# The second feed-forward product as 2x2x2 blocks with seven products

## The chip, the cores and the metric

The kernel runs on one core of one Trainium2 chip. The metric is device time in microseconds (us) of one execution, the median of several. Engine names are those of the profile: PE (matrix products), PEld (its weight loads), DVE (VectorE), ACT (ScalarE), POOL (GpSimd), SP (the engine that issues the DMAs).

## The reference

The reference computes one step of a two-layer streaming model on 1024 prompt tokens and 64 sample tokens, which the kernel puts side by side as T = 1088 columns. Layer 0 has a state-space mixer, layer 1 a banded attention that also makes shared keys and values. Behind each mixer stands the same gated feed-forward network, and the change lies in its second product, `... @ w_out`:

```python
def swiglu(u, w_in, w_out):
    g, up = jnp.split(u @ w_in, 2, axis=-1)
    return (jax.nn.silu(g) * up) @ w_out
...
        xp = xp + rmsnorm(swiglu(rmsnorm(xp, nw[2]), ffn_w_in[layer], ffn_w_out[layer]), nw[3])
```

The width of the model is 1024 (8 tiles of 128), the hidden width 2816 (FT = 22 tiles of 128).

## The kernel before

Activations lie with features on the 128 partitions and tokens in the columns. A float32 operand is split into a high part, rounded to the matrix engine's float32r format, and the low rest; a product is three matmuls (high by high, high by low, low by high). Tokens are cut in two ways: three slices SL of 384, 384 and 320 columns, and four quarters QS of 256, 256, 288 and 288. Two quarters make a half: b = 0 with 512 columns, b = 1 with 576.

`back` is everything behind a mixer's output, once per layer. Its first product (`plain_pairs`, `run_pair`) is already computed by blocks: for a pair of weight tiles (gate and up) and a half b, `run_pair` makes seven products P1 to P7 on operands of one quarter's width (256 columns for b = 0, 288 for b = 1). VectorE adds the results up from PSUM (L1328 to L1345), ScalarE takes the SiLU, GpSimd multiplies (L1342, L1346), and the hidden tile is written to the DRAM tensor `hd` (hscr in the rows). First come 6 pairs of half 0 without blocks, then 16 pairs with both halves, then 6 pairs with half 1 alone.

The second product is plain. For each slice s and each of 8 output tiles m it adds up 22 hidden tiles k, with three matmuls each (L1514 to L1516), in one PSUM tile. `loader` reads each hidden tile back from `hd` into a staging tile `sg` and splits it (ScalarE copies the high part, L1376; VectorE subtracts, L1377) into cells of the rings RX and R. The weights come through `Weights`: a DMA into one of two `raw` tiles or one tile lent from RX (L252), a ScalarE copy (L342), a VectorE subtraction (L343) into one of three `hl` tiles, which the matmuls read. An item of this plan is 8, 8 or 6 tiles of 128 columns. A `raw` tile can be loaded again when its item is split, and an `hl` tile is free again when its item's matmuls are done, so that the three `raw` and the three `hl` tiles form a ring.

At the end of a slice `end` scales (L1430), adds the residual from DRAM (x1d or x3d, L1386; L1431) and writes out. In layer 0 it then splits the result into the operands u of the next stage (L1447, L1448), sums squares (L1453 to L1455) and makes the slice's normalising row `rba`. The keys, queries and values of layer 1 (projections through `unit`, L467 to L469, two PSUM tiles `mm`) come next, slice by slice: V, K and Q of slices 0 and 1, K of a second head pair on both, and then slice 2. Their results leave PSUM through VectorE (L1679 vt, L1626 kf, L1652 qf).

PE's order is that of the program text, in which small generator tasks (`st.spawn`) are placed at estimated times. On the other engines and on SP a list scheduler fixes one static order, from priorities (`tc.high_priority`) and its own estimates; each engine then takes its instructions in that order.

## Time and profile before

| what | value |
|---|---|
| runs | 2938.93, 2940.55 and 2941.53 us (median 2940.55) |
| span of the profiled execution | 2929.9 us |
| outside the span, median less span | 10.65 us |
| first product, layer 0 and layer 1 | 912.7 to 1315.4 and 2250.1 to 2653.6 us |
| second product, layer 0 and layer 1 | 1315.4 to 1580.3 and 2653.6 to 2916.4 us |

The page gives no time of its own for the profiled execution besides the span, from the first instruction to the last; it is taken to have the same 10.65 us around it as the median run. A row of the view of stretches ("windows") has the stretch, its length, and for each engine the busy time and in brackets the number of instructions, then the granted clock of PE, the share of time in which the DMA engines were busy, and GB/s. A row of a view of groups has line, engine, operation, out<-in, shape and count, then busy time in us and mean ns of one, then idle time before them and what ended it. A row of DMA issues ends with KB each and the median us from issue to landing.

### The profile page before, as it was taken

What the parts mean: (1) busy time and instruction counts of PE and PEld (TensorE: products, weight loads), DVE (VectorE), ACT (ScalarE), POOL (GpSimd) and SP (SyncE); (2) the same over time, 40 slices, a digit from 0 to 9 for tenths busy, and PEclk for the clock granted to TensorE, in tenths of its full rate; (3) what the DMA queues carried; (4) which work ended last, traced back from release to release, by engine and by line L of the source; (5) the groups of instructions that cost most, each with busy time, mean ns of one, the idle gap of its engine ahead of it and who ended that gap; (6) DMA issues with size and microseconds to landing.
All of it is one profiled execution on the core that took longest, in us unless ns stands there. A gap on an engine that the chain in (4) does not pass through costs nothing.

```text
span 2929.9 us, 56271 instructions
## 1 busy us (share of the span) xinstructions
PE 2897.3 (99%) x21562; PEld 2858.7 (98%) x21562; DVE 2027.6 (69%) x4452; ACT 1403.6 (48%) x2535; POOL 718.9 (25%) x884
## 2 busy tenths in 40 slices
PE   8999999999999999999999999999999999999999
PEld 8999999999999999999999899999999999999998
DVE  7988878885867555583567887778688554575544
ACT  6655546454544222353445665556664222244443
POOL 1333333331022434350111000000131434351111
PEclk9999999999999999999999999999999999999999
DMA  4423333335564222345664322223476222245654
GB/s 138 133 92 106 104 98 109 100 117 165 165 187 137 76 81 77 108 151 163 207 192 154 98 74 72 65 69 108 132 204 179 83 77 81 75 154 178 225 171 135
DMA packets 203422, 369.12 MB, mean 126 GB/s; under 512 B 20752, under 2 KB 149488, under 8 KB 203152
## 3 DMA queue, kind: packets, MB, share of 16 engines
q1 hardware_dynamic: 199920, 354.97, 38.3%
q0 software_dynamic: 3232, 10.56, 2.0%
q8 instruction: 169, 2.77, 0.4%
q14 instruction: 101, 0.83, 0.1%
HBM read 298.24 MB, written 62.74 MB: 123 GB/s over the span
## 4 chain that ended last, share of the span: by engine, by line
PE 88%; DVE 6%; DMA 2%; ACT 2%; issue 1%; SPq 0%; POOL 0%; DVEq 0%; ACTq 0%; POOLq 0%
PE px L1314 9%; PE px L1315 9%; PE px L1313 9%; PE mm L467 8%; PE mm L469 8%; PE mm L468 8%; PE po L1515 6%; PE po L1516 6%; PE po L1514 6%; PE mmx L468 3%; PE mmx L469 3%; PE mmx L467 3%; PE ptp L1747 2%; PE po L1782 2%; PE S L1716 1%
## 5 line engine op out<-in xcount | busy, mean ns | idle before, releaser
L467 PE MATMUL mm<-r,hl 128*128 128x384 f32 (+2 forms) x1704 | 566.6, 333 | 2.6 <-DVE vt L1679 1.0
L469 PE MATMUL mm<-r,hl 128*128 128x384 f32 (+2 forms) x1704 | 549.6, 323 | 1.0 <-DVE hl L343 0.7
L468 PE MATMUL mm<-r,hl 128*128 128x384 f32 (+2 forms) x1704 | 549.3, 322 | 0.0
L343 DVE TENSOR_TENSOR hl<-raw,hl 128x1024 fp32r<-128x1024 f32 x216 | 256.3, 1187 | 216.6 <-ACT hl L342 208.9
L1314 PE MATMUL px<-r,hl 128*128 128x288 f32 (+1 forms) x1184 | 347.6, 294 | 0.0
L467 PEld LDWEIGHTS mm<-r,hl 128*128 128x128 f32 x1704 | 321.9, 189 | 4.9 <-DVE vt L1679 1.3
L469 PEld LDWEIGHTS mm<-r,hl 128*128 128x128 f32 x1704 | 321.1, 188 | 1.9 <-DVE hl L343 1.0
L468 PEld LDWEIGHTS mm<-r,hl 128*128 128x128 f32 x1704 | 322.2, 189 | 0.3
L1315 PE MATMUL px<-r,hl 128*128 128x288 f32 x1056 | 311.5, 295 | 0.0
L1313 PE MATMUL px<-r,hl 128*128 128x288 f32 x1056 | 310.4, 294 | 0.0
L342 ACT CAST hl<-raw 128x1024 fp32r<-128x1024 f32 x216 | 216.8, 1004 | 162.5 <-PE po L1516 101.6
L493 POOL TENSOR_TENSOR ssum<-ssum,sq 128x256 f32<-128x256 f32 (+3 forms) x97 | 125.5, 1295 | 616.9 <-ACT sq L492 601.3
L1314 PEld LDWEIGHTS px<-r,hl 128*128 128x128 f32 x1184 | 222.4, 188 | 0.0
L1315 PE MATMUL px<-rx,hl 128*128 128x256 f32 x768 | 214.2, 279 | 3.6 <-DVE hl L343 3.5
L1313 PE MATMUL px<-rx,hl 128*128 128x256 f32 x768 | 213.9, 278 | 0.4 <-DVE x L1290 0.4
L1515 PE MATMUL po<-rx,hl 128*128 128x384 f32 (+1 forms) x624 | 202.0, 324 | 0.2
L1313 PEld LDWEIGHTS px<-r,hl 128*128 128x128 f32 x1056 | 198.9, 188 | 0.1
L1315 PEld LDWEIGHTS px<-r,hl 128*128 128x128 f32 x1056 | 198.9, 188 | 0.0
L1514 PE MATMUL po<-rx,hl 128*128 128x384 f32 (+1 forms) x608 | 197.7, 325 | 0.0
L1516 PE MATMUL po<-rx,hl 128*128 128x384 f32 (+1 forms) x608 | 196.7, 324 | 0.0
L1314 PE MATMUL px<-rx,hl 128*128 128x256 f32 x640 | 178.4, 279 | 0.0
L1514 PE MATMUL po<-r,hl 128*128 128x384 f32 (+1 forms) x448 | 148.4, 331 | 0.0
(367 smaller groups left out, 7890.1 us busy)
## 6 DMA issues: line engine op xcount, KB each, us to landing
raw<-in_w_f_dram SPq DMA_DIRECT2D x154, 512.0 KB, 3.7
rx<-in_w_f_dram SPq DMA_DIRECT2D x54, 512.0 KB, 3.7
raw<-in_w_in_dram SPq DMA_DIRECT2D x40, 512.0 KB, 3.7
MT<-ascr SPq DMA_DIRECT2D x48, 384.0 KB, 4.3
sg<-hscr SPq DMA_DIRECT2D x88, 192.0 KB, 3.4
raw<-in_w_f_dram SPq DMA_DIRECT2D x44, 384.0 KB, 3.2
raw<-in_w_so_dram SPq DMA_DIRECT2D x32, 512.0 KB, 3.7
raw<-in_w_o_dram SPq DMA_DIRECT2D x19, 512.0 KB, 3.6
```

What stands on the lines that cost most here:

```text
L342: self.nc.scalar.copy(h, v)
L343: (eng or self.eng or self.nc.vector).tensor_tensor(lo, v, h, op=ALU.subtract)
L467: PE.matmul(ps[:, :n], h_, xh, start=(first and i == 0), stop=False)
L468: PE.matmul(ps[:, :n], h_, xl, start=False, stop=False)
L469: PE.matmul(ps[:, :n], l_, xh, start=False, stop=(last and i == nk - 1))
L493: (eng or G).tensor_tensor(ssum[:, :n], ssum[:, :n], q[:, :n], op=ALU.add)
L1313: PE.matmul(ps, wh, ah[:, k, :], start=(k == 0), stop=False)
L1314: PE.matmul(ps, wh, al[:, k, :], start=False, stop=False)
L1315: PE.matmul(ps, wl, ah[:, k, :], start=False, stop=(k == 3))
L1514: PE.matmul(ps[:, :n], wh, xh, start=(k == 0), stop=False)
L1515: PE.matmul(ps[:, :n], wh, xl, start=False, stop=False)
L1516: PE.matmul(ps[:, :n], wl, xh, start=False, stop=(k == FT - 1))
```

## The change

The second product is made by blocks too. The hidden tiles are paired: i and i + 11 (HF = 11) are the two halves of the inner dimension, even and odd output tiles the two halves of the output, and the two quarters of a half b those of the columns. Seven products (PROD2) with 11 inner tiles each and 4 output pairs g replace eight; P1, P6, P2 and P7 run on both halves with one load of the weights, P5, P4 and P3 on half 0 and then, with the weights loaded again, on half 1. `gate2` adds the PSUM results up in four SBUF tiles yq that hold the whole output.

The sums of hidden blocks are made in the first product, while the tiles are still in SBUF (`sum_one`, `sum_two`: four VectorE operations for each pair of tiles and half), and written to a new DRAM tensor hsm (hsum). The sums of weight blocks are made there too (`load_sums`, `sum_weights`: 24 jobs of four VectorE operations on 256 or 128 columns, two jobs at a time, loaded into z or an R tile and written to wsm, wsum). An order edge puts these sums behind a PSUM addition on VectorE and the weight loads behind the sums' DMAs on SP. In the second product the hidden tiles are loaded into their cells without a staging tile. A weight item is now 5 or 6 tiles; the low part of the item with 5 is made on GpSimd, the other on VectorE. The end works by quarters (`end`), and `end_slice` makes the operands of the next stage from two quarters.

```diff
+HF = FT // 2
+ORD = [i + HF * e for i in range(HF) for e in range(2)]
...
+WCH = ((6, 5), (0, 6))
...
-        for s in range(NSL):
-            for m in range(KD):
-                for k0, nk in KCH:
-                    W.plan(dict(src=[w2[m][:, k0 * P:(k0 + nk) * P]], n=nk * P))
-
-    KCH = ((0, 8), (8, 8), (16, 6))
...
+        for p_, x, y, _ in PROD2:
+            for g in range(4):
+                for k0, nk in WCH:
...
+                    W.plan(dict(src=[src], n=nk * P, eng=k0 > 0 and nc.gpsimd))
...
+    PROD2 = [
+        (P1, (0, 0), None, (0, 1)), (P6, None, 0, (0, 1)), (P2, (1, 0), None, (0, 1)), (P7, None, 3, (0, 1)),
+        *[(p_, x, y, (b,)) for b in range(2) for p_, x, y in ((P5, None, 2), (P4, None, 1), (P3, (1, 1), None))],
+    ]
...
+            def sum_weights(w, last):
...
+                for to, x, y, op in ((b22, b22, b12, SUB), (b12, b12, b11, SUB), (b11, b22, b11, ADD), (b21, b21, b11, SUB)):
+                    behind(V.tensor_tensor(to, x, y, op=op), last)
+                nc.sync.dma_start(wsm[:, :, g, c:c + n], z)
...
+            def sum_one(b, i, got, last=None):
...
+                behind(V.tensor_tensor(y0, got[0, 0], got[0, 1], op=SUB), last)
+                W.behind = nc.sync.dma_start(hsm[:, 0, i, BO[b] // 2:BO[b] // 2 + n], y0)
...
+                for j, to, x, y, op in ((2, y0, a22, y0, SUB), (1, y1, a21, a22, ADD), (3, y3, a12, y0, SUB)):
+                    behind(V.tensor_tensor(to, x, y, op=op), last)
+                    W.behind = nc.sync.dma_start(hsm[:, j, i, BO[b] // 2:BO[b] // 2 + ops[b].n], to)
...
+            for p_, _, _, bs in PROD2:
+                for g in range(4):
...
+                        for b in bs:
...
+                                PE.matmul(ps, wh, xh, start=(k0 > 0 and i == ks[0]), stop=False)
+                                PE.matmul(ps, wh, xl, start=False, stop=False)
+                                PE.matmul(ps, wl, xh, start=False, stop=(k0 == 0 and i == ks[-1]))
...
+                if len(bs) == 1 and p_ != P5:
+                    q = ((1, 2) if p_ == P4 else (0, 3))[bs[0]]
+                    st.spawn(end(q, yq[q], ssq[q], more[0]))
+                    if p_ == P3 and rb_out is not None:
+                        for s in ((0,), (1, 2))[bs[0]]:
+                            st.spawn(end_slice(s))
```

Three places show how the order moves. The first is SP in the first product of layer 0, over one pair of weight tiles with both halves. Before, from one raw load to the next but one (hscr are stores of hidden tiles u and c):

```order
L252 DMA raw<-in_w_f_dram 128x1024
L1343 DMA hscr_114<-u_13718 128x256
L1343 DMA hscr_114<-u_13733 128x288
L1347 DMA hscr_114<-c_13755 128x256
L252 DMA raw<-in_w_f_dram 128x1024
```

Now, on the same engine at such a pair (z and r are the loads of weight blocks to be summed, wsum and hsum the stores of the sums):

```order
L1406 DMA z<-in_w_f_dram 128x2x256 x2
L1406 DMA r<-in_w_f_dram 128x2x256 x2
L1444 DMA hscr_114<-u_12139 128x256
L1444 DMA hscr_114<-u_12154 128x288
L1444 DMA hscr_114<-c_12176 128x256
L260 DMA raw<-in_w_f_dram 128x1024
L1444 DMA hscr_114<-c_12192 128x288
L1415 DMA wsum_118<-z 512x1x256
L1415 DMA wsum_118<-r 512x1x256
L1473 DMA hsum_116<-y_12087 128x256
L1473 DMA hsum_116<-u_12139 128x256
```

Between two raw loads stand the stores of weight sums and of hidden sums, which wait for VectorE; four more hsum stores follow before the next raw load.

The second place is SP in the second product of layer 0. Before, at the end of slice 0, where that slice's result is written to x2d:

```order
L252 DMA rx<-in_w_f_dram 128x1024
L252 DMA raw<-in_w_f_dram 128x1024
L1433 DMA x2d<-y 128x2x384
L252 DMA raw<-in_w_f_dram 128x768
L1433 DMA x2d<-y 128x2x384 x2
L252 DMA rx<-in_w_f_dram 128x1024
```

Now, where the weights of P3 on half 0 are loaded (x1d is the residual, rx<-hsum a hidden sum read back):

```order
L1512 DMA r<-x1d 128x256 x2
L260 DMA rx<-in_w_f_dram 128x768
L1501 DMA rx<-hsum_116 128x288
L1512 DMA r<-x1d 128x256
L260 DMA raw<-in_w_f_dram 128x640
L1501 DMA rx<-hsum_116 128x288 x2
L260 DMA raw<-in_w_f_dram 128x768
L1512 DMA r<-x1d 128x256
L260 DMA rx<-in_w_f_dram 128x640
L1512 DMA r<-x1d 128x256 x2
L260 DMA raw<-in_w_f_dram 128x768
```

The items are smaller, and residuals and hidden tiles stand between nearly every two of them.

The third place is VectorE behind the second product of layer 0, up to the second `vt` (the values of slice 1 leaving PSUM). Before:

```order
L1652 SCALAR_TENSOR_TENSOR qf<-mm,rbf 128x384
L1431 TENSOR_TENSOR y<-y,r 128x320 x6
L1448 TENSOR_TENSOR r<-y,r 128x320 x2
L1634 TENSOR_TENSOR K_18538<-kf,K_18538 64x384
L1448 TENSOR_TENSOR r<-y,r 128x320 x6
L356 SCALAR_TENSOR_TENSOR hl<-raw,pcs,hl 128x128
L1634 TENSOR_TENSOR K_18539<-kf,K_18539 64x384
L1670 COPY Vn<-vtp 128x384
L1679 TENSOR_TENSOR vt<-mm,rbf 128x384
```

Now the last rows up to the same `vt`, which is line 1865:

```order
L536 SCALAR_TENSOR_TENSOR nr<-nv 128x3
L366 SCALAR_TENSOR_TENSOR hl<-raw,pcs,hl 128x128 x3
L1819 TENSOR_TENSOR K_19651<-kf,K_19651 64x384
L1584 TENSOR_TENSOR y<-y 128x4x32
L1819 TENSOR_TENSOR K_19652<-kf,K_19652 64x384
L1585 TENSOR_TENSOR y<-y 128x2x32
L1584 TENSOR_TENSOR y<-y 128x1152
L1865 TENSOR_TENSOR vt<-mm,rbf 128x384
```

Ahead of this piece the order now also has the last of quarter 2's end and the split and sums of slice 1 (19 subtractions into r and 6 scalings and additions more than before), which before were done a slice earlier; and the first sums of squares of slice 2 stand ahead of `vt` instead of behind it.

More of the change, by code (lines that the diff above doesn't have):

```diff
@@ L251, in load @@
         it["of"].append(ring)
-        self.nc.sync.dma_start(r[:, :it.get("n", 1024)], it["src"][len(it["raw"])])
+        self.loaded = self.nc.sync.dma_start(r[:, :it.get("n", 1024)], it["src"][len(it["raw"])])
+        if self.behind is not None:
+            self.tc.add_manual_dep(self.loaded.ins, self.behind.ins.name, ORDER, reason="place in the order")
         it["raw"].append(r)
@@ L1380, in end_load, with behind @@
-            def end_load(s):
-                o, n = SL[s]
-                xc = Cells(n, (R, 99)) if s == 2 else Cells(n, (RX, 99), (R, 99))
-                yield 0, EP_W[s] if s < 2 else 0, lambda: xc.room(KD)
+            hsm, wsm = hsm_[layer], wsm_[layer]
+            kept, summed, stored = {}, set(), set()
+            SUB, ADD = ALU.subtract, ALU.add
+            def behind(x, last):
+                if last is not None:
+                    tc.add_manual_dep(x.ins, last.ins.name, ORDER, reason="place in the order")
```

337 lines of the change are left out of this document (232 added, 105 removed).

## The prediction

> **What bounds the kernel now.** The page comes first: the span, the busy engines and the chain that ended last.
>
> ```profile
> span 2929.9 us, 56271 instructions
> ...
> PE 2897.3 (99%) x21562; PEld 2858.7 (98%) x21562; DVE 2027.6 (69%) x4452; ACT 1403.6 (48%) x2535; POOL 718.9 (25%) x884
> ...
> PE 88%; DVE 6%; DMA 2%; ACT 2%; issue 1%; SPq 0%; POOL 0%; DVEq 0%; ACTq 0%; POOLq 0%
> ```
>
> PE is busy 99% of the span and makes 88% of the chain. A change pays, then, by the PE time it takes out of a stage, less the waits it puts in. The view of stretches shows the stages that it touches.
>
> ```profile
> core 0: us, PE busy (x) PEld busy (x) DVE busy (x) ACT busy (x) POOL busy (x), PEclk, DMA share, GB/s
> ...
> 912.70:1315.40 402.70, 400.48 (x3196) 400.11 (x3195) 239.26 (x403) 140.07 (x230) 162.44 (x137) 1.00 0.31 97
> 1315.40:1580.30 264.90, 264.69 (x1610) 263.97 (x1609) 145.01 (x220) 121.27 (x198) 37.14 (x28) 1.00 0.59 185
> ...
> 2653.60:2916.40 262.80, 262.80 (x1598) 262.66 (x1598) 122.08 (x165) 103.78 (x160) 31.85 (x24) 1.00 0.57 181
> 2916.40:2929.90 13.50, 8.84 (x42) 6.12 (x40) 6.54 (x20) 3.42 (x8) 0.00 (x0) 1.00 0.28 97
> ```
>
> The second product lasts 264.9 and 262.8 us, with PE busy all through at clock 1.00. DVE, at 145 of 264.9 us, and the DMA engines, at 0.59, have room left. There is no wait to remove: only fewer or shorter matmuls help.
>
> **Term 1: the matmuls, −68 us.** The mean duration of a matmul is no measure, since they overlap. The step from one to the next is read from stretches that hold one shape: 384, 320, 288 and 256 columns, in this order.
>
> ```profile
> 1320.00:1400.00 80.00, 80.00 (x460) 80.00 (x459) 29.35 (x33) 31.34 (x48) 6.54 (x5) 1.00 0.51 159
> 2865.00:2915.00 50.00, 50.00 (x343) 50.00 (x342) 20.87 (x25) 17.08 (x24) 7.80 (x5) 1.00 0.46 141
> 1250.00:1310.00 60.00, 60.00 (x456) 60.00 (x455) 47.97 (x71) 27.03 (x43) 34.11 (x26) 1.00 0.45 142
> 655.00:690.00 35.00, 35.00 (x308) 34.98 (x307) 14.89 (x39) 14.35 (x30) 0.00 (x0) 1.00 0.39 125
> ```
>
> Length by count: 173.9, 145.8, 131.6 and 113.6 ns. A layer had 2 x 528 matmuls of 384 columns and 528 of 320 (8 outputs x 22 tiles x 3): 1056 x 173.9 + 528 x 145.8 = 260.6 us. It now has 7 products x 44 tile pairs x 3 = 924 of 256 and 924 of 288 columns: 924 x (113.6 + 131.6) = 226.6 us. That is 34.0 us less in each layer, 68 in all. The 2 to 4 us by which the stages exceed 260.6 (small matmuls of the ends) stay.
>
> The Trainium skill speaks against this term: "TensorE: Matmul & The Clock Gate", section "Back-to-back issue gap", gives a sustained step of about 81 ns at 128 columns and 131 at 512, so that narrow matmuls cost nearly what wide ones do. Drawn as a line (an estimate from that page) it makes 177 us before and 184 after, a loss of 8 us a layer. The rows above do not agree: 173.9 ns at 384 columns and 113.6 at 256 are in proportion to the columns.
>
> **Term 2: the weight ring while one half runs alone, +18 us (0 to +40).** In P1, P6, P2 and P7 one item of weights serves both halves: 16.5 matmuls x (113.6 + 131.6) = 4.0 us, about what an 8-tile item gave before (24 x 173.9 = 4.2 us). In P5, P4 and P3 an item serves one half: 1.87 us on half 0, 2.17 us on half 1. Three raw tiles turn round, so a turn (split, then load again) may take 5.6 us on half 0 and 6.5 on half 1. What a split takes, by the rows of the old second product on ScalarE and VectorE, and GpSimd's in the first product:
>
> ```profile
> L342 ACT CAST hl<-raw 128x768 fp32r<-128x768 f32 x22 | 18.4, 837 | 0.0
> ...
> L343 DVE TENSOR_TENSOR hl<-raw,hl 128x768 fp32r<-128x768 f32 x22 | 21.8, 989 | 24.9 <-ACT hl L342 24.6 <-ACT sq L492 0.3
> ...
> L343 POOL TENSOR_TENSOR half<-raw,half 128x512 fp32r<-128x512 f32 x18 | 24.9, 1385 | 0.0
> ```
>
> 6 tiles (768 columns): 0.84 + 0.99 = 1.8 us. 5 tiles: 0.72 + 1385 x 640/512 = 2.4 us. Mean 2.1. The load depends on what else the DMA engines carry; a calm and a loaded stretch, each with its 384 KB loads:
>
> ```profile
> 1370.00:1400.00 30.00, 30.00 (x174) 30.00 (x173) 10.31 (x11) 12.03 (x19) 2.59 (x2) 1.00 0.42 128
> ...
> raw<-in_w_f_dram SPq DMA_DIRECT2D x3, 384.0 KB, 3.1
> ...
> 1400.00:1420.00 20.00, 20.00 (x117) 19.97 (x116) 13.63 (x21) 11.30 (x21) 2.44 (x2) 1.00 0.86 278
> ...
> r<-x1d SPq DMA_DIRECT2D x8, 192.0 KB, 6.0
> ...
> raw<-in_w_f_dram SPq DMA_DIRECT2D x1, 384.0 KB, 4.4
> ```
>
> What will the load be? Half 0 alone lasts 3 x 132 x 113.6 ns = 45 us and reads 24 items (8.7 MB), by the order some 24 hidden tiles (3.5 MB) and the first residuals (about 1 MB): 290 GB/s, like the stretch with 278 GB/s and share 0.86. A turn is then 2.1 + 4.4 us and an allowance of 0.5 us, half an operation, for waiting behind other work on a busy engine: 7.0 us, 1.4 too long on half 0 and 0.5 on half 1. Each has 8 turns: 11 + 4 us, less 3 for the two turns that are in stock when the phase begins, and less about 3 because a PE that waits asks for less: 9 us a layer, 18 in all. With the calm load a turn is 5.7 us and the term about 0. With a load near the 6.0 us of the x1d row the turn is 8.6: 24 + 17 us, but slower consumption then lightens the load; I take 20 a layer as the end.
>
> The Trainium skill, "DMA: Bandwidth & Descriptors", section "Specifications", puts the HBM limit of a core at about 358 GB/s. By it 290 GB/s would fit and the term would be 0; the row shows landings lengthening from 3.1 to 4.4 us at 278 GB/s already, and a ring of three waits for landings.
>
> **Term 3: VectorE behind layer 0's second product, +10 us (2 to 14).** Before, the stretch behind it reads:
>
> ```profile
> 1590.00:1600.00 10.00, 10.00 (x60) 9.97 (x60) 9.82 (x23) 6.18 (x16) 0.00 (x0) 1.00 0.32 108
> 1600.00:1610.00 10.00, 9.01 (x54) 8.65 (x53) 9.51 (x22) 5.76 (x12) 0.00 (x0) 1.00 0.28 76
> ...
> L1430 DVE SCALAR_TENSOR_TENSOR y<-y,pcs,rb 128x320 f32<-128x320 f32 x8 | 3.8, 544 | 0.2 <-ACT rb L533 0.2
> L1448 DVE TENSOR_TENSOR r<-y,r 128x320 fp32r<-128x320 f32 x8 | 3.4, 482 | 0.0
> ...
> 1602.83 0.56 DVE L1679 TENSOR_TENSOR vt<-mm,rbf 128x384 f32<-128x384 f32 x1
> ...
> 1603.45 0.44 PE L467 MATMUL mm<-r,hl 128*128 128x384 f32 x1 [0.99 <-DVE vt L1679]
> ```
>
> VectorE is full there, and PE has just begun to wait: with two PSUM tiles `mm`, Q of slice 1 cannot start before V of slice 1 has left PSUM, 23 us behind the stage's end. The new order puts 6 scalings and additions (about 0.5 us each), 19 subtractions of 256, 128 or 32 columns (11 x 0.4 + 8 x 0.2), some 8 sums (4 us) and two more chains of small normalising operations (3 us) ahead of that `vt`, and 6 weight scalings fewer (−2 us): about 14 us more on a full engine. PE's wait of 1 us grows by up to 14. Some of it comes back, since the sums that followed `vt` are then done. I take 10. The last product of half 1 ends the layer with VectorE near full too: in its three products (52 us) I count 11 splits of 0.99, 16 PSUM additions of 0.46 and the ends of two and a half quarters, about 52 us.
>
> **Term 4: the first product, +4 us (0 to 10).** Per pair with both halves PE works 84 x (113.6 + 131.6) = 20.6 us. VectorE's share and what the sums cost:
>
> ```profile
> 950.00:1240.00 290.00, 290.00 (x2340) 290.00 (x2340) 151.50 (x270) 86.03 (x144) 111.38 (x98) 1.00 0.26 84
> 1245.00:1315.00 70.00, 70.00 (x533) 70.00 (x532) 57.49 (x89) 36.15 (x59) 37.44 (x28) 1.00 0.48 152
> ...
> L308 DVE TENSOR_TENSOR tt<-tt,raw 128x512 f32<-128x512 f32 x19 | 13.9, 731 | 9.9 <-POOL tt L290 8.5 <-DMA raw<-in_w_f_dram 1.4
> ...
> L1377 DVE TENSOR_TENSOR rx<-sg,rx 128x320 fp32r<-128x320 f32 x17 | 8.0, 502 | 3.9 <-ACT rx L1376 3.8
> ```
>
> It is busy 10.8 us of a pair. The sums add 4 of hidden tiles (0.45 us, between these rows in size) and 8 of weights (0.4): 15.8 of 20.6 us. On SP some 12 issues are added, and the DMA rate rises from 84 GB/s by 2.1 MB of weight blocks and 0.6 MB of sums per pair to about 215. What hides them is PE's own work of 20.6 us, with six PSUM tiles of 1.4 us or more each in flight. The risk is an addition from PSUM behind a sum that waits for GpSimd's product or for z; were the cover gone, one such wait of 0.5 us per pair in 22 pairs and two layers would cost 22 us. The orders place the sums behind P6 and P2 additions, so I take 4. In the last stretch (half 1 alone) VectorE goes from 57.5 to about 62 of 70 us: the hidden sums are new, the prefetch splits are narrower.
>
> **Term 5: the tail, −1 us.** The last 13.5 us now handle 288 columns instead of 320.
>
> **Sum.** −68 + 18 + 10 + 4 − 1 = −37. The profiled execution spans 2929.9 us and is taken as a run like the median one, 10.65 us longer outside: 2940.55 − 37 = 2904.
>
> **The rivals.** (a) *The ring keeps up*: DVE at 145 of 264.9 us and DMA at 0.59 speak for it; terms 1, 3, 4 and 5 remain, 2885. (b) *Slower: the ring decides.* A layer loses 8 x (T − 5.6) + 8 x (T − 6.5) for a turn T. Against 34 us less 7 for terms 3 to 5, it is lost from T = 7.7 us on, which a load of 5.1 us gives; at T = 9 the loss is 47 us a layer and the time 2940.55 − 68 + 94 + 13 = 2980. The 6.0 us of x1d speaks for it, that a waiting PE asks for less speaks against. (c) *The first product stalls* by the 22 us of term 4: 2922. That VectorE has about 5 of 20.6 us left speaks against it. (d) *The step does not shrink with the columns*: had the narrow matmuls the old mean step, 260.6/1584 = 164.5 ns, 1848 of them take 304 us, +43 a layer: 2940.55 + 87 + 31 = 3058. The step rows exclude it almost wholly; the page quoted under term 1 is a milder form. (e) *The change doesn't take out what it says*: excluded by the order, which has 1848 matmuls of the stated widths per layer.
>
> **How the numbers follow.** Forecast 0.50; (a) 0.25; (b) 0.10; (c) 0.13; (d) 0.02. The range takes in (a), (c) and the bounds of the terms: low −68 + 2 − 1 = −67 us, 2874, high −68 + 40 + 14 + 10 = −4 us, 2936. A measurement of this kernel tells about 0.2% (6 us) from no change. Faster takes the forecast, (a), (c) but for a little: 0.85. Within 0.2%: 0.05, the edge between the forecast and (b). Slower: 0.10.
>
> **What would show it right or wrong.** In the new profile, the second product should last 227 us plus PE waits released by hl (ACT, DVE or POOL) inside P5, P4 and P3, most on half 0, with a DMA share near 0.9; none in P1 to P7's shared part. Behind layer 0, PE should wait for `vt` of slice 1. The first product should stay within 10 us of 402.7. Steps of 256 columns above 114 ns would break term 1; a calm ring would break term 2; a second product over 255 us would make it rival (b).

## The result: 1.3% slower

| | before | after |
|---|---|---|
| median of 4 runs | 2939.74 us | 2977.69 us |
| lowest to highest | 2936.74 to 2941.53 | 2971.28 to 2979.52 |
| ratio, 95% interval | | 1.0127 [1.0112, 1.0141] |
| span of the profiled execution | 2929.9 us | 2969.5 us |

The forecast was 2904 us, in a range of 2874 to 2936. The profiled execution of the new kernel took 2971.28 us, only 1.8 us more than its span: the 10.65 us that the prediction put around the span were mostly the distance between a low run and the median. That moves the level, not the difference.

The page of the new kernel, as the prediction began with: span, busy time, and the shares of the chain that ended last.

```profile
span 2969.5 us, 59291 instructions
...
PE 2868.1 (97%) x22094; PEld 2810.0 (95%) x22094; DVE 2268.2 (76%) x5126; ACT 1424.6 (48%) x2744; POOL 851.9 (29%) x980
...
PE 7%; DVE 2%; issue 2%; DMA 2%; POOL 1%; ACT 0%; SPq 0%; DVEq 0%; POOLq 0%; ACTq 0%
```

PE lost only 29 us of busy time, where 68 were to go, and it now stands idle for 101 us of the span instead of 33. The shares of the chain add up to only 14%, so this chain was followed back over the last 400 us or so, and it can't be set against that of before. The stretches do: first product, second product, the same in layer 1, and the tail.

```profile
914.60:1334.40 419.80, 405.28 (x3194) 400.77 (x3193) 322.65 (x574) 132.94 (x231) 167.65 (x138) 1.00 0.51 165
1334.40:1591.10 256.70, 240.04 (x1867) 234.53 (x1866) 167.82 (x335) 131.15 (x285) 92.32 (x70) 0.98 0.68 208
2278.30:2700.20 421.90, 405.61 (x3195) 400.93 (x3194) 330.81 (x578) 138.61 (x237) 167.76 (x138) 1.00 0.51 164
2700.20:2952.10 251.90, 238.46 (x1864) 234.20 (x1863) 155.19 (x301) 120.28 (x249) 90.70 (x69) 0.99 0.68 210
2952.10:2969.50 17.40, 10.67 (x46) 7.73 (x44) 8.72 (x26) 3.24 (x8) 1.15 (x1) 0.84 0.32 109
```

| stage (first to last matrix product, us) | before | after | change | forecast |
|---|---|---|---|---|
| up to the first product | 912.7 | 914.6 | +1.9 | 0 |
| first products, layers 0 and 1 | 402.5, 403.2 | 419.8, 421.8 | +35.9 | +4 |
| second products | 264.7, 262.6 | 256.7, 251.9 | −18.7 | −50 |
| between the layers | 670.2 | 687.2 | +17.0 | +10 |
| tail | 13.8 | 17.2 | +3.4 | −1 |

The first product, where DVE went from 239 to 323 us of busy time, lost more than the second gained. PE's longest groups of waits in the first product of layer 0, in its second product and in the 109 us behind it (what waits, who releases it; total us, times, longest):

```profile
PE px L1338 <- DVE u L1353: 4.2, 6, 1.4
PE px L1340 <- DVE hl L353: 4.0, 3, 1.9
PE px L1338 <- DVE p L1355: 2.7, 3, 1.1
...
PE po L1705 <- DVE hl L353: 8.7, 10, 2.6
PE po L1705 <- POOL hl L353: 4.0, 6, 1.2
PE po L1703 <- ACT hl L352: 2.2, 2, 1.7
...
PE nbp L542 <- DVE nr L536: 4.2, 2, 3.9
PE mm L481 <- DVE hl L366: 3.5, 2, 2.3
PE nst L512 <- POOL ssum L505: 3.0, 1, 3.0
```

Nearly all are released by DVE or POOL. In the first product u and p are additions from PSUM, which the prediction named as the risk; hl are splits of weights; nr and ssum belong to the normalising rows. None is released by `vt`.

### The profile page after: what moved, and what is told of

Its sections match the earlier page's. It is cut to its first block, busy times and chain, and to the rows that moved or that the text cites. A ratio compares the mean times of both kernels' runs of the same rounds, so it can differ in the third digit from the quotient of the medians.

```text
span 2969.5 us, 59291 instructions
## 1 busy us (share of the span) xinstructions
PE 2868.1 (97%) x22094; PEld 2810.0 (95%) x22094; DVE 2268.2 (76%) x5126; ACT 1424.6 (48%) x2744; POOL 851.9 (29%) x980
## 5 line engine op out<-in xcount | busy, mean ns | idle before, releaser
L353 DVE TENSOR_TENSOR hl<-raw,hl 128x1024 fp32r<-128x1024 f32 (+1 forms) x174 | 202.4, 1164 | 130.6 <-ACT hl L352 129.7
L352 ACT CAST hl<-raw 128x1024 fp32r<-128x1024 f32 (+2 forms) x226 | 208.0, 921 | 133.4 <-PE po L1705 54.3
L1705 PE MATMUL po<-r,hl 128*128 128x288 f32 (+1 forms) x696 | 204.1, 293 | 16.4 <-DVE hl L353 11.9
L1703 PE MATMUL po<-r,hl 128*128 128x288 f32 (+1 forms) x696 | 202.1, 290 | 0.0
L1704 PE MATMUL po<-r,hl 128*128 128x288 f32 (+1 forms) x696 | 201.4, 289 | 0.0
L1338 PEld LDWEIGHTS px<-rx,hl 128*128 128x128 f32 x768 | 145.5, 190 | 16.8 <-DVE u L1353 14.9
L1703 PE MATMUL po<-rx,hl 128*128 128x256 f32 (+1 forms) x536 | 155.6, 290 | 5.0 <-ACT hl L352 4.3
```

The costliest lines, as they stand in the source:

```text
L352: self.nc.scalar.copy(h, v)
L353: (eng or self.eng or self.nc.vector).tensor_tensor(lo, v, h, op=ALU.subtract)
L1338: PE.matmul(ps, wh, ah[:, k, :], start=(k == 0), stop=False)
L1703: PE.matmul(ps, wh, xh, start=(k0 > 0 and i == ks[0]), stop=False)
L1704: PE.matmul(ps, wh, xl, start=False, stop=False)
L1705: PE.matmul(ps, wl, xh, start=False, stop=(k0 == 0 and i == ks[-1]))
```

## The experiments

Times of single runs of one kernel scatter by some 13 us (k1 below: 2925.24 to 2938.01 in ten runs). Stage lengths scatter less: where two kernels (k1 and f5) were profiled twice, a stage differs by up to 2 us between the two profiles and the tail by up to 3 us, while the second product and the stretch behind it together repeat within 0.4 us. So the stages are read, and times only where a kernel was timed several times ("rounds"); all the others are single runs. In the rows with rounds the time is a median and the span that of one profiled run. "Before" is the kernel before on the same chip.

| run | us (before) | span | first products | second products | between | tail |
|---|---|---|---|---|---|---|
| e1_sums_at_p2 | 2955.43 (2937.49) | 2952.6 | 413.2, 410.5 | 257.4, 249.8 | 687.6 | 16.6 |
| e2_no_weight_sums | 2962.22 (2937.49) | 2959.9 | 412.3, 410.3 | 259.7, 254.9 | 688.9 | 16.8 |
| e3_no_hidden_sums | 2948.30 (2937.49) | 2946.6 | 409.8, 412.1 | 256.3, 248.6 | 687.0 | 16.9 |
| e6_both_halves | 2968.80 (2937.49) | 2967.1 | 421.3, 420.3 | 234.2, 232.8 | 718.9 | 20.5 |
| e4_four_raw_tiles | 2965.07 (2943.89) | 2963.0 | 420.4, 422.2 | 253.8, 244.7 | 686.9 | 17.1 |
| e5_low_parts_on_vectore | 2951.28 (2943.89) | 2949.4 | 420.5, 422.5 | 245.6, 243.9 | 687.3 | 15.0 |
| e7_p3_by_halves | 2957.87 (2943.89) | 2956.2 | 411.9, 410.3 | 238.8, 240.2 | 719.4 | 17.9 |
| e8_e7_later_prefetch | 2957.84 (2943.89) | 2956.1 | 412.5, 411.9 | 240.3, 238.2 | 718.3 | 17.9 |
| e9_filled_waits | 2957.09 (2937.76) | 2955.4 | 410.5, 410.0 | 255.5, 250.8 | 694.5 | 16.9 |
| k1_p2_sums_low_parts | 2931.39 (2937.76) | 2929.7 | 414.2, 410.7 | 245.5, 241.5 | 687.2 | 14.7 |
| f5_p5_both_halves | 2930.81 (2937.76) | 2929.1 | 410.4, 410.7 | 256.2, 238.4 | 679.8 | 18.0 |
| d1_no_low_parts_of_u | 2924.03 (2937.98) | 2922.3 | 412.8, 410.2 | 241.5, 240.9 | 683.4 | 15.9 |
| g2_slice0_first, rounds | 2938.18 (2937.98) | 2935.8 | 413.7, 411.2 | 246.8, 245.6 | 687.6 | 17.0 |
| k1_timed, rounds | 2932.10 (2937.63) | 2933.1 | 413.9, 410.4 | 246.3, 241.9 | 686.6 | 17.6 |
| f5_timed, rounds | 2929.38 (2937.63) | 2926.2 | 411.8, 411.0 | 256.8, 236.3 | 679.6 | 16.9 |

### The first product: sums that run beside GpSimd

The prediction priced a weight sum (L1414, 128x256) at 0.4 us. The timeline of DVE in one pair of the new kernel, and POOL's over the same time (start, duration, instruction):

```profile
1028.18 0.44 DVE L1370 TENSOR_TENSOR u<-px,u 128x288 f32<-128x288 f32 x1
1028.54 1.15 DVE L1414 TENSOR_TENSOR z<-z 128x256 f32<-128x256 f32 x1
...
1030.49 1.51 DVE L1414 TENSOR_TENSOR z<-z 128x256 f32<-128x256 f32 x1
...
1032.88 0.41 DVE L1414 TENSOR_TENSOR z<-z 128x256 f32<-128x256 f32 x1
...
1027.66 1.75 POOL L301 TENSOR_TENSOR tt<-raw 128x512 f32<-128x512 f32 x1
1029.36 0.93 POOL L1371 TENSOR_TENSOR c<-p,u 128x256 f32<-128x256 f32 x1
1030.25 1.48 POOL L353 TENSOR_TENSOR half<-raw,half 128x512 fp32r<-128x512 f32 x1
1031.68 0.99 POOL L1371 TENSOR_TENSOR c<-p,u 128x288 f32<-128x288 f32 x1
```

The same sum takes 1.51 us while POOL works and 0.41 us from 1032.88 on, when POOL has stopped; the addition L1370, with one operand in PSUM, takes 0.44 us beside POOL. If that is what the first product pays for, calling the sums at another place of the pair, behind P2, must bring it back.

```diff
+                    if p_ == P2:
+                        for w in workers:
+                            if "job" in w:
+                                sum_weights(w, last)
...
-                elif p_ == P3:
-                    for w in workers:
-                        if "job" in w:
-                            sum_weights(w, last)
```

> The weight sums of the first product are moved from behind P3, where GpSimd is busiest (tt, c and half one behind the other), to behind P2, where GpSimd is idle; the same instructions and the same DMAs. Changed kernel: 96 sums a layer (L1414), 72 us of VectorE in layer 0, single ones of 128x256 between 0.41 and 1.5 us; first product 419.8 and 421.8 us. Theory A (a VectorE operation with two SBUF operands is slowed by a GpSimd operation that runs beside it): the sums fall to 0.41 to 0.6 us each, about 40 us a layer, and the first product to 405 to 410 us, 10 us or more less in each layer. Theory B (the amount of work on VectorE and SP, wherever it stands): sums unchanged or the first product within 3 us of 420.

The weight sums fell to their price without GpSimd. The group of L1414 in the new kernel (first two rows) and in this one:

```profile
L1414 DVE TENSOR_TENSOR z<-z 128x256 f32<-128x256 f32 x48 | 42.0, 876 | 0.2 <-DMA z<-in_w_f_dram 0.2
L1414 DVE TENSOR_TENSOR r<-r 128x256 f32<-128x256 f32 x32 | 21.3, 665 | 0.0
```

```profile
L1414 DVE TENSOR_TENSOR z<-z 128x256 f32<-128x256 f32 x48 | 19.9, 415 | 0.0
L1414 DVE TENSOR_TENSOR r<-r 128x256 f32<-128x256 f32 x32 | 13.3, 416 | 0.0
```

The first products shrank by 6.6 us in layer 0, where 10 or more were expected, and by 11.3 in layer 1; the span by 16.9. In layer 0 part of the gain was lost again: other VectorE sums, the 128x512 ones of the prefetch (L318, L319), now run beside GpSimd in their turn and went from 0.86 to 1.26 and from 1.07 to 1.29 us on the mean. The Trainium skill, "SBUF — State Buffer", section "Who interferes with whom", says that only the pair of ports that VectorE and GpSimd share makes them contend, under an exclusive lock, and that a VectorE instruction with two SBUF inputs contends with a GpSimd instruction that reads SBUF, while one with at most one SBUF input does not. The 1.51 us beside a POOL instruction of 1.48 us, and L1370's 0.44 us, agree.

Is it only the place, or the sums themselves? Two kernels leave one kind out each:

```diff
-                elif p_ == P5 and len(ops[1].hl) == len(OPI):
+                elif p_ == 99 and len(ops[1].hl) == len(OPI):
...
-                        src = wsm_[layer][:, y, g, k0 * P:(k0 + nk) * P]
+                        src = w2[2 * g][:, k0 * P:(k0 + nk) * P]
```

> The weight sums are left out: no loads of z and r, no sums, no stores wsum; the products that read sums read plain weights instead, so that the output is not the reference's. The second product has the same loads, splits and matmuls. Theory A (weight sums slow the first product): first product 404 to 408 us in each layer instead of 420 and 422. Theory C (the hidden sums and their stores slow it): 414 us or more. Second product unchanged within 3 us (256.7 and 251.9) in both.

```diff
-                y0 = got["y0"] = (box[0] if e else tmp_[0]).tile([P, n], F32, tag=f"y0{e}", name="y0")
-                behind(V.tensor_tensor(y0, got[0, 0], got[0, 1], op=SUB), last)
+                y0 = got["y0"] = got[0, 0]
...
-                    behind(V.tensor_tensor(to, x, y, op=op), last)
```

> The hidden sums on VectorE are left out (4 operations per pair of tiles and half), their stores to hsum remain and write plain hidden tiles, so that the output is not the reference's. Theory A (weight sums): first product 416 to 420 us, at most 4 us less. Theory C (hidden sums): 410 us or less.

Without weight sums the first products are 412.3 and 410.3: neither of the two expectations was met, but it is as with the sums moved, so that once away from GpSimd's work the weight sums cost nothing measurable. Without hidden sums the first products are 409.8 and 412.1 although the weight sums stay slow; this was a miss, 416 to 420 was expected. So neither kind is dear alone. The weight sums stand behind P3's additions and the hidden sums right after them, behind P6's and P2's of the next pair. That only both together, one of them stretched, hold up the additions from PSUM is what these three runs suggest; no wait was followed to show it.

Some 7 to 8 us a layer remain in each of these kernels: the last six pairs take 73 to 75 us, where the kernel before takes 66.6 and 66.8, whatever was left out. All of these kernels kept the stores of hidden sums on SP, and the order edges that weight loads wait for there; no run took those out, and the cause stays open.

### The weight ring: what waits in P5, P4 and P3

In the new kernel P6, P2 and P7 take within 0.3 us of 132 x (113.6 + 131.6) = 32.4 us each, which is what term 1 says; P1 takes 36.1 and 35.7 us, with waits. P5, P4 and P3 exceed their matmuls by 25.8 us in layer 0 and 21.3 in layer 1: 8.6 and 8.7 of them on half 0, 17.2 and 12.6 on half 1. To see whether it is the weights' supply, these three run on both halves too:

```diff
-        *[(p_, x, y, (b,)) for b in range(2) for p_, x, y in ((P5, None, 2), (P4, None, 1), (P3, (1, 1), None))],
+        *[(p_, x, y, (0, 1)) for p_, x, y in ((P5, None, 2), (P4, None, 1), (P3, (1, 1), None))],
```

> P5, P4 and P3 of the second product run on both halves with one load of the weights, like P1, P6, P2 and P7: 56 items of weights a layer instead of 80, the same matmuls and hidden loads; quarters 1 and 2 end together, then 0 and 3. Ring theory (a weight item that serves one half is used up faster than three raw tiles can be split and loaded again): the 26 and 21 us of waits in P5 to P3 fall below 5 us, second product 230 to 236 us a layer instead of 256.7 and 251.9. Rival (VectorE's work for the ends, residual loads and stores make the waits): second product 245 us or more. In both, the stage behind layer 0 and the tail get longer, 5 to 15 us each, since two quarters end at once.

The excess falls to 3.1 and 2.9 us and the second products to 234.2 and 232.8, as expected. That fits the supply, but does not show it alone: the edit also takes the ends of the quarters, which are work for VectorE too, out of the products on half 1. And 31.7 us come back behind layer 0, where 5 to 15 were expected, since the quarters now end two by two, 1 and 2 behind P4 and then 0 and 3 behind P3. In this kernel, PE's longest wait, and then 40 us about the end of the product:

```profile
PE nst L512 <- DVE ssum L1586: 17.7, 2, 14.2
```

```profile
1564.00:1604.00 40.00, 14.49 (x102) 13.11 (x100) 35.58 (x113) 21.10 (x65) 5.33 (x9) 0.70 0.46 148
```

What in the supply? The prediction said the turn of three raw tiles. A fourth one:

```diff
-            phase[0], W.lent.cap = 2, 1
+            phase[0], W.lent.cap = 2, 2
```

> One tile more is lent to the weights in the second product, so that four raw tiles turn round instead of three; nothing else is changed in the program. Changed kernel: 26 and 21 us of waits in P5 to P3 (a turn takes 6.7 us on half 0 and 8.7 and 8.1 on half 1, three items' matmuls 5.6 and 6.5). Ring theory with the load as the long part: four items' matmuls are 7.5 and 8.7 us, the waits fall to 12 us or less a layer. Rival (a late split, since VectorE and GpSimd come late to it): a loaded tile more doesn't help, waits stay above 20 and 16 us.

The excess fell to 23.2 and 14.8 us only, 2.6 and 6.5 us less, where 12 or less was expected: the turn is a part. The other candidate is the split itself, whose second half GpSimd did:

```diff
-                    W.plan(dict(src=[src], n=nk * P, eng=k0 > 0 and nc.gpsimd))
+                    W.plan(dict(src=[src], n=nk * P, eng=None))
```

> The low part of every weight item of the second product is made on VectorE, none on GpSimd (40 subtractions of 640 columns a layer change engine). If GpSimd's time for them (1.65 us each, against about 0.8) and its slowing of VectorE's own operations make the ring late: waits in P5 to P3 fall by 10 us or more a layer, and VectorE's splits of 768 columns come down from 1.08 and 1.31 us to about 0.97. If the amount of work on VectorE makes it late: waits grow, most on half 1 of layer 0.

The splits of the new kernel in the second product, 1465 to 1580 us, and then those of this kernel:

```profile
L353 DVE TENSOR_TENSOR hl<-raw,hl 128x768 fp32r<-128x768 f32 x14 | 15.3, 1093 | 11.6 <-ACT hl L352 11.6
L353 DVE TENSOR_TENSOR hl<-rx,hl 128x768 fp32r<-128x768 f32 x8 | 10.5, 1309 | 2.6 <-ACT hl L352 2.3 <-ACT rx L1502 0.3
...
L353 POOL TENSOR_TENSOR hl<-raw,hl 128x640 fp32r<-128x640 f32 x15 | 24.8, 1650 | 31.2 <-ACT hl L352 27.7 <-DVE nv L533 3.5
```

```profile
L353 DVE TENSOR_TENSOR hl<-raw,hl 128x768 fp32r<-128x768 f32 x16 | 15.6, 972 | 7.5 <-ACT hl L352 7.5
L353 DVE TENSOR_TENSOR hl<-raw,hl 128x640 fp32r<-128x640 f32 x15 | 12.8, 854 | 2.6 <-ACT hl L352 2.6
```

One engine less, and faster: 5 tiles take 0.85 us on VectorE instead of 1.65 on GpSimd, and VectorE's own 6 tiles fall from 1.09 and 1.31 to 0.97. Second products 245.6 and 243.9, 11.1 and 8.0 us less. In P5, P4 and P3 the excess falls by 8.5 us to 17.3 in layer 0 and by 7.7 to 13.7 in layer 1, less than the 10 or more that was expected. GpSimd's help had cost VectorE 4.4 us on its own 22 splits of that stretch (15.3 + 10.5, against 22 x 0.972), and each 5-tile item 0.8 us of its turn.

So 31.0 of the 47.1 us stay in this kernel. The two edits, e4's and e5's, were not run together, and what remains was not divided. In layer 0 the longest wait left is not for weights at all:

```profile
PE nst L512 <- POOL ssum L505: 4.9, 1, 4.9
```

PE waits 4.9 us there for GpSimd's sums of squares, the end of a quarter.

### Behind layer 0: latency, clock or load

Two kernels with the sums at P2 keep half 0 and half 1 together in P5 and P4 and part P3 alone; they also start slice 1's operands ahead of slice 0's. The second of them also starts the prefetch of hidden tiles 14 us later (against the wait in the last six pairs).

```diff
+        (P5, None, 2, (0, 1)), (P4, None, 1, (0, 1)), (P3, (1, 1), None, (0,)), (P3, (1, 1), None, (1,)),
...
-                        st.spawn(loader())
+                        st.spawn(loader(), 14.0)
```

> Weight sums behind P2 as in the first experiment, and P5 and P4 on both halves with one load of the weights, so that only P3 runs by halves; quarters 1 and 2 end behind P4, quarter 0 behind P3 on half 0, quarter 3 last. Ring theory: no waits in P5 and P4 (under 1 us each), at most 8 us in P3, second product 232 to 240 us; the stage behind layer 0, 687 us in the changed kernel and 719 with both halves throughout, comes to 685 to 695 us and the tail to 13 to 14 us. The span then is 2910 to 2930 us, at or below that of the kernel before (2930). Rival (the ends' work on VectorE costs the same wherever it stands): what the second product gains comes back behind it, span 2945 us or more.

> As the one before, with the first hidden tiles' loading begun 14 us later in the stretch of the first product where half 1 runs alone. There PE waits for weight splits 8 us a layer, while VectorE does the last hidden sums and a burst of 14 hidden splits. If the burst is what delays the weight splits: the six pairs of half 1, 74.4 us together in the first experiment, fall to 70 us or less (66.3 is their matmuls). If not: within 1 us of 74.

Second products of 238.8 and 240.2, about as expected (232 to 240), but the span stayed at 2956: the stretch behind took 719 us, where 685 to 695 were expected, with slice 0's operands (r) late. The waits there:

```profile
PE mm L480 <- DVE r L1579: 15.3, 2, 12.1
```

The later prefetch changed nothing clear of scatter. That leaves the ends of the quarters, an inference which is tested next. One row of the kernel before, then one of the new one: the 40 us behind the second product of layer 0.

```profile
1580.00:1620.00 40.00, 39.01 (x235) 38.54 (x234) 33.22 (x84) 22.15 (x54) 1.75 (x7) 1.00 0.44 132
```

```profile
1591.00:1631.00 40.00, 29.51 (x141) 28.05 (x140) 37.12 (x117) 23.85 (x68) 3.41 (x6) 0.83 0.33 111
```

PE was busy 39 of 40 us and is now busy 29.5; DVE is at 37.1; and the granted clock, 1.00 through the whole region before, is 0.83. Three suspects: chains of latencies, the clock, and VectorE's load. The clock first. In the new kernel's last product of half 1 it goes to about a half where PE has just waited 2.56 us for a split:

```profile
1564.00:1570.80 6.80, 5.34 (x37) 4.71 (x36) 6.44 (x8) 3.26 (x5) 4.58 (x3) 1.00 0.82 261
1570.80:1577.60 6.80, 4.58 (x18) 4.23 (x19) 5.51 (x11) 1.56 (x4) 1.18 (x3) 0.53 0.69 223
```

The timeline there, of PE and then of the split that it waits for, with GpSimd's beside it:

```profile
1571.91 0.61 PE L1705 MATMUL po<-r,hl 128*128 128x288 f32 x1 [2.56 <-DVE hl L353]
...
1569.58 2.28 DVE L353 TENSOR_TENSOR hl<-raw,hl 128x768 fp32r<-128x768 f32 x1
...
1569.46 1.58 POOL L353 TENSOR_TENSOR hl<-raw,hl 128x640 fp32r<-128x640 f32 x1 [0.36 <-ACT hl L352]
```

The split took 2.28 us beside GpSimd's, where it takes 0.97 with no such help from GpSimd (e5).

The experiment fills three of the waits with idle products (in the kernel with the sums at P2):

```diff
+        for _ in range(fill):
+            PE.matmul(sp[:, :P], ones, ones, start=True, stop=True)
...
+        for _ in range(fill):
+            PE.matmul(bp[:, :P], ones, ones, start=True, stop=True)
```

> Edit on top of the kernel with the weight sums moved to the second product P2 (span 2952.6, 687.6 us between layer 0's second product and layer 1's first): 12, 28 and 34 idle 128-column products of ones (0.11 us each at the full clock, 8 us in all) stand in TensorE's order where it waited 1.8, 3.1 and 4.1 us in that kernel: ahead of the transposed sums of the third and fourth quarter and ahead of slice 1's broadcast row. They are overwritten; nothing of the result changes. Theory A: TensorE's granted clock falls to 0.5 because TensorE stood idle, and these three waits bring three of the five half-clock stretches (6.8, 3.4, 3.4 us of 23.8) behind layer 0; with the waits filled those go and the stretch takes 680 to 683 us. Rival B: the half clock is not due to the waits but to the heavier use of the engines or the DMA; the stretches stay and the time between stays at 687 to 690, or grows where the idle products are late.

The 40 us behind the second product, without and with the filling:

```profile
1587.80:1627.80 40.00, 29.16 (x140) 27.89 (x139) 36.65 (x116) 23.63 (x67) 3.07 (x6) 0.83 0.33 107
```

```profile
1583.00:1623.00 40.00, 35.20 (x235) 34.49 (x234) 36.55 (x117) 23.51 (x66) 3.39 (x8) 0.91 0.35 112
```

The clock rose from 0.83 to 0.91, so it does fall because PE waits. No time came back: second product and stretch together took 950.0 us instead of 945.0. But this run can't judge the clock, since the filling itself held PE up. The idle products took 17.1 us, not the 8 that were planned, and ran past the end of two of the three waits. In this kernel (the sums ssum and the row nr, and the products that need them):

```profile
1587.88 2.15 POOL L505 TENSOR_TENSOR ssum<-ssum,sq 128x288 f32<-128x288 f32 x1 [3.93 <-ACT sq L504]
1587.02 6.42 PE L511 MATMUL nst<-ones 128*128 128x128 f32 x56
1593.27 0.49 PE L514 MATMUL nst<-ident,ssum 128*128 128x128 f32 x3
...
1618.97 0.15 DVE L538 SCALAR_TENSOR_TENSOR nr<-nv 128x3 f32<-128x3 f32 x1
1616.07 7.86 PE L544 MATMUL nbp<-ones 128*128 128x128 f32 x68 [0.65 <-DVE nv L525]
1623.76 0.49 PE L546 MATMUL nbp<-ident,nr 128*128 128x128 f32 x3
```

ssum was ready at 1590.03 and nr at 1619.12, but PE came to them 3.2 and 4.6 us later: 7.8 us, more than the 5.0 that were lost. An estimate without this overrun is 942 us, 3 below 945.0. So what the clock costs stays open; at 0.83 over 40 us it is at most 40 x (1 − 0.83) = 6.8 us, so it can't be the whole of the 17.0.

The load next; DVE is at 36.6 of 40 us in both kernels. In k1_p2_sums_low_parts (below) 14 us of VectorE's work are taken out, some of it behind the product:

```diff
-                            V.tensor_tensor(ul[:, c], y[:, m, :], uh[:, c], op=ALU.subtract)
+                            A.copy(ul[:, c], y[:, m, :])
```

> The kernel k1_p2_sums_low_parts (span 2929.7, between 687.2) with one change: the low parts of layer 1's attention inputs (128x288 and smaller, 0.28 to 0.45 us each on VectorE, 40 of them or 14 us in all for the three slices) are not computed as differences on VectorE; ScalarE writes a copy of the value in their place, so that part of the computation is left out. Theory A (behind layer 0's second product VectorE, busy 36.3 of 40 us there, is what TensorE waits for): some 10 us of its work go between the last quarter and slice 1's row; between 675 to 681, span 2918 to 2924. Rival B (a chain of single latencies or the clock sets the restart, not VectorE's load): between 685 to 690.

Second product and stretch took 924.9 us instead of 932.7, 7.8 less. The stretch alone fell to 683.4, between the two expectations; 4.0 of the gain lie in the last product on half 1, although PE waits 5.3 us there for ScalarE's casts (0.7 in k1), since ScalarE now makes the copies. So VectorE's load is a cause; that it is the whole of it wasn't shown.

### Putting it together

> Two edits at once: the weight sums at P2 instead of P3 (alone: 16.9 us off the span) and the low parts of the second product's second weight half on VectorE instead of GpSimd (alone: 20.1 off). Theory A, the two costs are apart (first product; weight ring of the second): first products 412 and 411, second products 246 and 244, between 687, tail 10.5: span 2969.5-16.9-20.1 = 2932 to 2938. Rival B: both lean on VectorE's idle time, and VectorE with both is the bound again: first products over 416 or second products over 250, span 2944 or more.

The two edits, e1 and e5, add up: span 2929.7, against 2932 to 2938 expected. The span is 39.8 us shorter than the new kernel's, as much as the change had lost (39.6). P5 on both halves goes on top, with P4 and P3 still by halves and shorter delays of the normalising steps:

```diff
-        *[(p_, x, y, (b,)) for b in range(2) for p_, x, y in ((P5, None, 2), (P4, None, 1), (P3, (1, 1), None))],
+        (P5, None, 2, (0, 1)),
+        *[(p_, x, y, (b,)) for b in range(2) for p_, x, y in ((P4, None, 1), (P3, (1, 1), None))],
...
-EP_W, ER_W, EQ_W = (4.0, 9.4, 2.0, 2.2), (8.9, 8.9, 5.0, 3.3), (11.0, 4.0)
+EP_W, ER_W, EQ_W = (2.0, 2.0, 2.0, 2.2), (6.0, 6.0, 5.0, 5.0), (1.0, 2.0)
```

> The two edits of the previous kernel, and P5 multiplied for both halves at once while P4 and P3 stay by halves, half 0 first (so that half 0's quarters still end early), with the delays of the normalising steps shortened so that their rows stand spread over TensorE's order. Theory A (the ring lacks time only where one half runs alone, and the late ends cost only where all quarters end together): second products 238 to 241, between 682 to 692, tail 10 to 13, first products 411: span 2918 to 2930, under the kernel before. Rival B (whatever shortens the second product comes back behind it, since the residual, the normalising rows and the next slices' splits set the restart there): between 700 to 720, span 2940 to 2955.

Layer 1 did as expected (238.4 us), layer 0 did not (256.2), though the stretch behind it was the shortest of these kernels (679.8; 670.2 before the change). Its last product waits for slice 0's sums, while VectorE is busy 33.6 of 37 us. In this kernel, the wait and then the stretch:

```profile
PE nst L512 <- DVE ssum L1587: 17.6, 2, 10.2
```

```profile
1550.00:1587.00 37.00, 18.80 (x116) 17.95 (x115) 33.59 (x97) 20.49 (x59) 5.00 (x9) 0.72 0.51 162
```

Order or load? The same work with slice 0 first (this edit, like f5's own, is shown against the new kernel; against f5 it also puts one delay, EQ_W's first, from 1.0 to 6.0):

```diff
-LDP, WTP, ENP, ENS, ATP = 1500, 2200, (0, 0, 1800, 1500), (0, 1800, 1500), 1000
+LDP, WTP, ENP, ENS, ATP = 1500, 2200, (2500, 2500, 1800, 1500), (2500, 1800, 1500), 1000
...
-EP_W, ER_W, EQ_W = (4.0, 9.4, 2.0, 2.2), (8.9, 8.9, 5.0, 3.3), (11.0, 4.0)
+EP_W, ER_W, EQ_W = (2.0, 2.0, 2.0, 2.2), (6.0, 6.0, 5.0, 5.0), (6.0, 2.0)
```

> The kernel f5_p5_both_halves (span 2929.1; in it TensorE stood 18 us inside layer 0's last product, since the transposed sums of slice 0 stand there in its order while VectorE, busy 33.6 of 37 us, did the third quarter's residual and slice 1's splits first) with two changes of order: on VectorE the ends of quarters 0 and 1 and slice 0's splits and sums go ahead of the third quarter's end and of slice 1, and slice 0's transposed sums stand 42 products later on TensorE. Theory A (only VectorE's order was wrong): the 18 us go, the second product of layer 0 takes 238 to 242, between stays at 680 to 695, span 2912 to 2922. Rival B (VectorE is full there, so whatever goes first, something else is late): the second product shrinks but the time between grows by as much, sum 930 to 938 as before (256.2+679.8 = 936.0), span 2925 to 2932.

The wait for the sums is gone, and the splits of weights are late instead.

```profile
PE po L1706 <- DVE hl L353: 9.0, 2, 5.6
```

246.8 + 687.6 = 934.4 us against 936.0, which agrees with the load as the limit. But the edit puts these ends ahead of the splits (2500 against 2200), so that late splits follow from the order too, and layer 1's second product became 7 us longer (245.6, 238.4 in f5): this order gains nothing, and that no other does is not shown. Its ratio to the kernel before is 1.0005 [0.9996, 1.0015]. The other two kernels were then timed several times:

> The kernel k1_p2_sums_low_parts again, timed in rounds: its one look gave 2931.39 beside 2937.76 of the kernel before. Theory A (the two edits take 37 of the 39.6 us back, and the product's 30 fewer us of matmul steps are given back behind layer 0 and in the tail): 2933 to 2938, ratio to before 0.998 to 1.000. Rival B (the look was a low one): 2939 or more, no gain over before.

> The kernel f5_p5_both_halves again, timed in rounds: its one look gave 2930.81 beside 2937.76; its second product and the stretch behind it sum to 936.0, those of k1_p2_sums_low_parts to 932.7, the kernel with slice 0 put first to 934.4 at a ratio of 1.0005. Theory A (the three are one kernel within the measurement, since VectorE is full behind layer 0 in each): 2932 to 2939, ratio 0.998 to 1.000. Rival B (P5 on both halves is worth its own 8 us a layer): 2928 or less, ratio 0.996 or less.

k1: 2932.10 us, ratio 0.9983 [0.9973, 0.9993]. f5: 2929.38 us, ratio 0.9973 [0.9962, 0.9984], which is 0.27% below the kernel before. It is the lowest of the kernels that compute everything, but its runs (2925.04 to 2933.80) overlap k1's, and the two are not told apart. Its second products:

```profile
1325.50:1582.40 256.90, 234.33 (x1867) 232.87 (x1866) 181.47 (x402) 133.09 (x296) 29.81 (x31) 0.96 0.65 201
...
2673.10:2909.30 236.20, 231.71 (x1863) 230.13 (x1862) 159.57 (x332) 115.35 (x241) 28.92 (x29) 1.00 0.69 212
```

Of the 68 us of matmul steps this kernel keeps 34 in the second products (256.8 + 236.3 against 527.3) and pays 17 in the first, 9 between the layers and 3 in the tail.

## Why the prediction was wrong

In spans the change was forecast at −37 us and measured at +39.6, 76.6 apart: 31.9 of them in term 4, 31.3 in the second products (term 2), 7.0 in term 3, 4.4 in term 5 and 1.9 ahead of the first product. Two steps failed, terms 4 and 2. Each left its own bounds; with either of them right and all else as measured, the change would still be about +8 us, above the upper end of −4.

- **Term 1, −68 us: right.** P6, P2 and P7 last what 113.6 and 131.6 ns a step give, within 0.3 us.
- **Term 4, +4 us (0 to 10): the first failed step, +35.9.** It is the price of the sums: "The sums add 4 of hidden tiles (0.45 us, between these rows in size) and 8 of weights (0.4)". The weight sums took 0.88 us in z and 0.67 in r, up to 1.5 us singly, because the prices were taken from rows without asking whether GpSimd, busy 111 of 290 us in that stage, ran beside them. "15.8 of 20.6 us" left no room for that, least of all between a pair's P3 and the next pair's P2, where the sums of both kinds stand. Moving the weight sums freed 17.9 us (e1). Another 14.6 us (8.1 and 6.5) lie in the last six pairs and have no known cause, though the prediction put them under the same cover.
- **Term 2, +18 us (0 to +40): the second failed step, right place, too small: 47.1 us over the matmuls in P5, P4 and P3.** The price of a turn was wrong. It was to come from the load: half 0 alone at 290 GB/s and 4.4 us for a landing, most waits on half 0. Half 0 alone ran at 239 GB/s with a DMA share of 0.76 and landings of 3.2 to 3.9 us, and 29.8 of the 47.1 us lie on half 1. What the prediction left out is what GpSimd's split does to VectorE's: 1.09 and 1.31 us beside it, 0.97 without, and once 2.28. Taking it off GpSimd frees 8.5 and 7.7 us there (e5), a fourth raw tile 2.6 and 6.5 (e4). Of the 31.0 us that remain in e5, 4.9 are a wait for sums of squares; the rest was not divided.
- **Term 3, +10 us (2 to 14): sign right, +17.0, another mechanism.** PE does not wait for `vt` but for normalising rows, POOL's square sums and scaled weight splits. "Full engine" was right: DVE at 37.1 of 40 us, and 7.8 us back for 14 us of its work removed (d1), 3.8 of them in this stretch. The half clock that follows the waits comes on top, with at most 6.8 us; its price was not measured. Missing was that quarters 2 and 3 now end one product on half 1 apart (132 x 131.6 ns = 17 us), where the slices before ended 528 x 145.8 ns = 77 us or more apart, so that their ends crowd into one stretch; e6 and e7 crowd more and lose 32 us.
- **Term 5, −1 us: +3.4.** No run was made on it, and two profiles of one kernel (k1) differ by 2.9 us in the tail.
- **The signs it named.** The second product of layer 0, at 256.7 us, is over the 255 that were to mean rival (b), and layer 1's, at 251.9, is not; P1 has waits, where none were to be; the first products left their 10 us; no wait is for `vt`; the DMA share stayed below 0.9 (0.76 with half 0 alone).
- **The rivals.** (b), slower by the ring, and (c), the stall of the first product, happened together: each was priced as if it came alone and got 0.10 and 0.13. They share a cause, VectorE beside GpSimd (e1 and e5), so their chances were not independent. The upper end of the range took 10 us for term 4, though the text itself had worked out 22 for "one such wait of 0.5 us per pair"; even with 22 it would have ended at about 2949, below the 2977.69 measured.

The prices that term 4 missed stood in the trace of the kernel before. It has two VectorE sums of one shape, 128x512 with both operands in SBUF: L308, 0.73 us on the mean, which the prediction shows, and L309, 1.02 us. In that kernel, L309 beside GpSimd's L291 (1061.64 to 1063.38), and L308 while GpSimd does nothing (1077.76 to 1079.34):

```profile
1061.27 0.96 DVE L309 TENSOR_TENSOR tt<-raw,tt 128x512 f32<-128x512 f32 x1
1077.79 0.69 DVE L308 TENSOR_TENSOR tt<-tt,raw 128x512 f32<-128x512 f32 x1 [0.45 <-POOL tt L290]
```

## What to carry to other kernels

When a change trades matrix products for element-wise sums, price every sum by what runs beside it: a row of the same shape under the same neighbours, not the cleanest row. Ask where in the loop the new work lands, not how full the engine is on average: here the weight sums were free at one place of a pair and cost 7 to 11 us a layer at another. And an earlier end of a stage is worth only what the engine behind it can take up: two orders (e6, e7) made layer 0's second product 19 to 23 us shorter and lost 32 us behind it, where VectorE was nearly full (35.6 of 40 us in e6).

## What was not expected of the hardware

- A VectorE operation with both operands in SBUF took 0.41 us alone and 0.96 to 1.51 us beside GpSimd's; with one operand in PSUM, 0.44 us beside it.
- After a wait of 2.56 us in an otherwise busy stretch the granted clock was 0.53 over 6.8 us. Idle products in three such waits raised it from 0.83 to 0.91 over 40 us. They held PE up themselves, by 7.8 us, so what the clock cost stays open.
